# A planner's view of part-tile transfers, the adaptive sums' first term and bias, and the last mixed rows, in a two-layer hybrid DiT kernel on one core

## The chip, the cores and the metric

The kernel runs on one core of a Trainium2 chip. Its time is the device time of one execution in microseconds (us), taken as the median of several runs; a kernel before and a kernel after the change are timed on the same chip. The profile that is read below comes from one further execution with the hardware profiler on.

TensorE is PE in the rows (its weight loads are PEld), VectorE is DVE, ScalarE is ACT, GpSimd is POOL and SyncE is SP. A "q" behind an engine's name (SPq, ACTq) marks the engine's own issuing of DMAs, as against its computing.

## The reference, cut to what matters

Two layers run on 256 latent tokens of width 2048; 256 context tokens join in layer 0. All data are float32.

```python
def reference(x, c, ctx, c_ctx, ada_w, ada_b, norm_g, na_ssd_w_in, ...):
    for i in range(2):
        shift, scale, gate = adaln(c, ada_w[i], ada_b[i])     # silu(c) @ ada_w + ada_b, 3 x 2048
        h = modulate(rms_norm(x, norm_g[i]), shift[:, None], scale[:, None])
        if i == 0:                                            # the context is modulated likewise
            y = na_ssd_mixer(h, hc, ...)                      # one 2048-wide input projection,
                                                              # attention and SSD heads, a group norm,
                                                              # one output projection of [ya, yb]
        else:
            y = short_conv_mixer(h, sc_w_in, sc_conv_w, sc_w_out)
        x = x + gate[:, None] * y
    return x

def short_conv_mixer(h, w_in, conv_w, w_out):
    bg, cg, hv, g = jnp.split(h @ w_in, 4, axis=-1)
    y = bg * dw_conv(cg * hv, conv_w)                         # 3 taps along the tokens
    return (jax.nn.silu(g) * y) @ w_out
```

## The kernel before

**The main stream.** Nearly all of the work is matrix products with weights that are read once. SP brings each weight in pieces of 512 KB into raw buffers (L393). ACT rounds a piece to the short float format of the fast matmul (the CAST to wH, L423), DVE subtracts to get the rest (the TENSOR_TENSOR to wL, L430), and PE multiplies wH by the high and the low part of the activations and wL by the high part (all matmuls are recorded at L198). There are three wH and three wL buffers and five raw ones. A raw buffer is free once its wL is made, and the next load into it is issued then. In layer 1 a piece is worth twelve matmuls of 128x512: eight with wH, four with wL.

**The side work.** Everything else (norms, attention, SSD, convolutions, gates) is written as Python generators that hand out one instruction or a few at a time, in three queues: urgent, side and back. While the kernel is built, a planner (`Plan`, L45 to L135) keeps a clock for each engine and an end time for each written and read piece of a tile, from a table of estimated costs. Before each weight's matmuls, `pump` (L291) asks `may` (L263) for each generator whether the data of its next step would be there in time by these clocks, and if so the step is written into the program at that place. So the planner's clocks set the order in which each engine will execute; on the chip an engine works through its list in that order, and an instruction whose data are late holds up all behind it on its engine. For a DMA, `Plan.add` (L98) takes the start as no earlier than the end of the earlier write to the same piece of the output tile, and sets that piece's end time anew.

**Transfers that fill a tile in parts.** Three places fill one tile by several DMAs: `fetch` (L208 to L213), which reads a 128x2x512 tile by four DMAs of 32 partitions each from the DRAM array trd into Du or Dg, on ACT's queue; the four loads of the attention bias at L1018; and the two loads of exr rows into one tile at L1332. Du and Dg serve layer 1: for each of four column groups `row_gen` (L1755) computes cg * hv, writes it to trd, fetches it back as Du in an order that DVE's 32x32 transposes (`blocks`, L217) turn into channel-major u, and then does the convolution: four multiplications on ACT (L1783) and eight multiply-adds on DVE (L1787, L1789) into v. `gate_gen` (L1793) does the same for the gate with Dg and cg, and multiplies into v and y (L1826 to L1831).

**The adaptive sums.** `gemv_gen` (L805 to L846), in the back queue, computes sixteen blocks of 512 of silu(c) @ ada_w + ada_b on DVE, between the weights. For each block it clears acc (128x512, L810), lets SP put the bias into acc's first row (L811), then adds sixteen products of 512 columns (L820; two per 512 KB piece of ada_w, which uses a raw buffer like a weight). PE sums over the partitions with a matrix of ones, and DVE copies the result to rowb (L829), which ACT's queue writes to the DRAM array mrow.

**The mixed rows.** Layer 0's two head groups make 32 tiles of 128x256. `put_mix` (L936) writes each to the DRAM array mixd on ACT's queue; `mix_gen` (L1528) reads them back two at a time when the room of the old activations is free, and splits them into a high part (ACT) and a low part (DVE) for the output projection. In the group norm, `group_gen` brings the scale r2 (one value per token on the partitions) into a row for all channels: DVE builds two diagonal matrices dg, and PE multiplies ones by them.

## Time and profile before

| | |
|---|---|
| Median of the runs | 1802.93 us (1802.58 to 1804.87, 3 runs) |
| The profiled execution's own time | 1802.22 us |
| Its span, first to last instruction | 1800.3 us |
| Mean granted TensorE clock | 0.998 |
| DMA | 385.23 MB, mean 214 GB/s |
| ACT busy | 785.7 us (44%) |
| POOL busy | 31.1 us (2%) |

The page of the profile gives busy times, the span in 40 slices, and the chain of work that ended last. From the trace behind it come the groups of instructions (count, mean duration, and what ended the idle time before them), the waits by engine, the timeline of a stretch (start, duration, engine, line, operation, the count of instructions drawn together in the row, and in brackets the idle time ahead with what ended it), and the busy times and clock in stretches of one's choice. PE loses 29.3 us in gaps of over 0.3 us between its matmuls; 12.7 us of it is the first load.

### The profile page before, as it was taken

How to read it: one execution, taken by the hardware profiler on the slowest of the kernel's cores; microseconds unless marked ns; L12 is line 12 of the kernel's file. 1: busy time of each engine (PE TensorE's matmuls, PEld its weight loads, DVE VectorE, ACT ScalarE, POOL GpSimd, SP SyncE). 2: the span in 40 equal slices, each digit the busy share in tenths (PEclk: the TensorE clock that was granted, in tenths of full speed). 3: DMA queues.
4: the chain of work that ended last, by engine and by line, in shares of the span. 5: the costliest groups of instructions: out<-in, count | busy, mean ns of one | idle time of the engine just before them, and what ended most of it. 6: DMA issues, size and time to landing. Idle time of an engine off the chain costs nothing.

```text
span 1800.3 us, 25545 instructions
## 1 busy us (share of the span) xinstructions
PE 1760.2 (98%) x9545; PEld 1469.2 (82%) x9545; DVE 1283.5 (71%) x2049; ACT 785.7 (44%) x1354; POOL 31.1 (2%) x28
## 2 busy tenths in 40 slices
PE   6999999999999999999999999999999999999998
PEld 4677888889888879888878898788877888878887
DVE  5566777878686867685875787787657777767555
ACT  5323544436252455242454343554445444434442
POOL 0000100001000000000001000000000000000000
PEclk9999999999999999999999999999999999999999
DMA  9987654576656556655574566768757888878774
GB/s 347 340 291 254 194 168 126 156 206 194 211 161 190 162 174 204 191 158 167 172 219 120 163 188 194 232 209 295 273 184 232 260 278 268 270 237 265 220 220 167
DMA packets 260220, 385.23 MB, mean 214 GB/s; under 512 B 33424, under 2 KB 113008, under 8 KB 260096
## 3 DMA queue, kind: packets, MB, share of 16 engines
q1 hardware_dynamic: 239792, 366.64, 64.8%
q10 hardware_dynamic: 20304, 16.96, 3.1%
q8 instruction: 75, 1.23, 0.3%
q14 instruction: 49, 0.40, 0.1%
HBM read 372.89 MB, written 11.96 MB: 214 GB/s over the span
## 4 chain that ended last, share of the span: by engine, by line
PE 89%; DMA 4%; DVE 4%; issue 1%; ACT 1%; SPq 0%; POOL 0%; ACTq 0%; POOLq 0%; DVEq 0%
PE bank L198 86%; PE bank L202 3%; DMA raw<-in_ada_w 2%; DVE wL L430 2%; DMA tmp<-dram_csr 1%; DVE acc L820 0%; DMA raw<-in_w_in 0%; DMA Dg<-dram_trd 0%; ACT wH L423 0%; DMA tmp<-in_x 0%; DMA xs<-in_x 0%; DVE hL L769 0%; DVE tmp L1398 0%; DVE tmp L1217 0%; DMA Du<-dram_trd 0%
## 5 line engine op out<-in xcount | busy, mean ns | idle before, releaser
L423 ACT CAST wH<-raw 128x1024 fp32r<-128x1024 f32 (+1 forms) x440 | 459.5, 1045 | 707.4 <-PE bank L198 606.5
L430 DVE TENSOR_TENSOR wL<-raw,wH 128x1024 fp32r<-128x1024 f32 (+1 forms) x440 | 530.5, 1212 | 225.9 <-ACT wH L423 224.1
L198 PE MATMUL bank<-hH,wH 128*128 128x256 f32 (+1 forms) x1040 | 342.7, 330 | 0.9 <-ACT wH L423 0.9
L198 PE MATMUL bank<-hL,wH 128*128 128x256 f32 (+1 forms) x1040 | 336.8, 324 | 0.0
L198 PE MATMUL bank<-hH,wL 128*128 128x256 f32 (+1 forms) x1024 | 331.3, 324 | 1.5 <-DVE wL L430 1.5
L198 PE MATMUL bank<-wH,h 128*128 128x512 f32 x1024 | 318.7, 392 | 2.1 <-DVE h L1662 1.7
L198 PE MATMUL bank<-wH,hH 128*128 128x512 f32 x640 | 257.2, 402 | 4.8 <-ACT hH L763 2.6
L820 DVE SCALAR_TENSOR_TENSOR acc<-raw,csil,acc 128x512 f32<-128x512 f32 x256 | 191.7, 749 | 91.0 <-DMA raw<-in_ada_w 74.0
L198 PE MATMUL bank<-wL,hH 128*128 128x512 f32 x640 | 249.8, 391 | 0.3 <-DVE wL L430 0.3
L198 PE MATMUL bank<-wH,hL 128*128 128x512 f32 x640 | 249.5, 390 | 0.1
L198 PEld LDWEIGHTS bank<-wH,h 128*128 128x128 f32 x1024 | 193.0, 189 | 44.3 <-DVE h L1662 3.0
L198 PEld LDWEIGHTS bank<-hH,wH 128*128 128x128 f32 x1040 | 197.6, 190 | 18.7 <-issue 2.0
L198 PEld LDWEIGHTS bank<-hL,wH 128*128 128x128 f32 x1040 | 197.7, 190 | 15.6
L198 PEld LDWEIGHTS bank<-hH,wL 128*128 128x128 f32 x1024 | 194.5, 190 | 17.8 <-DVE wL L430 2.5
L198 PE MATMUL bank<-wL,h 128*128 128x512 f32 x512 | 200.7, 392 | 5.4 <-DVE wL L430 5.4
L198 PE MATMUL bank<-wH,mix 128*128 128x512 f32 x512 | 162.7, 393 | 0.0
L198 PEld LDWEIGHTS bank<-wH,hH 128*128 128x128 f32 x640 | 120.2, 188 | 35.3 <-issue 6.5
L198 PEld LDWEIGHTS bank<-wH,hL 128*128 128x128 f32 x640 | 120.1, 188 | 25.6 <-DVE hL L769 0.6
L198 PEld LDWEIGHTS bank<-wL,hH 128*128 128x128 f32 x640 | 120.2, 188 | 24.8 <-DVE wL L430 1.1
L198 PEld LDWEIGHTS bank<-wL,h 128*128 128x128 f32 x512 | 96.6, 189 | 27.1 <-DVE wL L430 6.9
L198 PEld LDWEIGHTS bank<-wH,mix 128*128 128x128 f32 x512 | 96.1, 188 | 20.8 <-issue 0.9
L198 PE MATMUL bank<-wL,mix 128*128 128x512 f32 x256 | 99.8, 390 | 0.0
(257 smaller groups left out, 1754.4 us busy)
## 6 DMA issues: line engine op xcount, KB each, us to landing
raw<-in_w_in SPq DMA_DIRECT2D x209, 512.0 KB, 3.8
raw<-in_ada_w SPq DMA_DIRECT2D x163, 512.0 KB, 4.7
raw<-in_sc_in SPq DMA_DIRECT2D x128, 512.0 KB, 4.4
raw<-in_w_out SPq DMA_DIRECT2D x64, 512.0 KB, 4.8
raw<-in_sc_out SPq DMA_DIRECT2D x32, 512.0 KB, 4.6
tmp<-dram_csr SPq DMA_DIRECT2D x32, 256.0 KB, 6.2
PT<-in_ada_w SPq DMA_DIRECT2D x14, 512.0 KB, 8.0
yi<-in_ada_w SPq DMA_DIRECT2D x8, 512.0 KB, 7.4
```

The source lines that it names most:

```text
L198: E(T.matmul(o, l, r, start=start, stop=stop, skip_group_check=True))
L202: E(T.transpose(o, i, ident if k == 128 else ident[:k, :k]))
L423: E(S.copy(H, v))
L430: E(V.tensor_tensor(out=Lo, in0=v, in1=H.bitcast(F32), op=ALU.subtract))
L820: E(V.scalar_tensor_tensor(out=acc, in0=v[:, j], scalar=csil[:, 2 * k + j:2 * k + j + 1], in1=acc, op0=ALU.mult, op1=ALU.add))
```

## The change

The diff has five parts.

1. In `Plan.add` a DMA no longer waits in the plan for the earlier write of the same piece, and the piece's end is the later of both. The four DMAs of a fetch or of a bias tile and the two of an exr tile are planned beside each other instead of one after the other.
2. An engine's name may end in "+" (`may`): the data then count as ready 2000 ns later. Used for the products of acc ("DVE+") and for the reading back of mixed rows ("ACT+").
3. `gemv_gen`: no clearing of acc and no bias in acc. The bias goes to a tile adab of its own (128 partitions, four rows used, cleared once), the first product of a block is a TENSOR_SCALAR that writes acc, and the bias is added where the sum leaves its bank for rowb (a TENSOR_TENSOR in place of a COPY).
4. `put_mix` puts a tile straight into its final place (`place`) when the room is free already: eight of the 32 tiles. `mix_gen` reads the others back.
5. `group_gen`: dg and its two matmuls with ones are replaced by two transposes of r2 broadcast to 128x128.

```diff
@@ -105,7 +105,7 @@
         for k in ki:
             s = max(s, self.w[k] + 60)
         for k in ko:
-            s = max(s, 0.0 if e == "PE" else self.w[k] + 60, self.r[k] + 60)
+            s = max(s, 0.0 if e == "PE" or op == "DMACopy" else self.w[k] + 60, self.r[k] + 60)
         if op == "DMACopy":
             n = 4
             for _, c in outs[0].ap:
@@ -128,7 +128,7 @@
             self.r[k] = max(self.r[k], free)
             self.last[k[0]] = max(self.last[k[0]], free)
         for k in ko:
-            self.w[k] = done
+            self.w[k] = max(self.w[k], done) if op == "DMACopy" else done
             self.last[k[0]] = max(self.last[k[0]], done)
         return b
 
@@ -268,8 +268,10 @@
             return grow(task)
         if nb and len(free_b) < nb + (0 if isurg else reserve[0]):
             return False
+        late = eng[-1] == "+"
+        eng = eng.rstrip("+")
         now, t = plan.t["PE"], plan.t["ACT" if eng == "AQ" else eng]
-        rdy = plan.ready(aps)
+        rdy = plan.ready(aps) + (2000 if late else 0)
         if eng == "AQ":
             return t <= now + hor and rdy <= t
         if hor < 2000 and nb and sorted(plan.last[b.tensor.name] for b in free_b)[nb - 1] + 3000 > now:
@@ -329,7 +331,7 @@
                     else:
                         if len(free_b) < nb:
                             continue
-                        when_ = max(plan.t["ACT" if eng == "AQ" else eng], plan.ready(f))
+                        when_ = max(plan.t["ACT" if eng == "AQ" else eng.rstrip("+")], plan.ready(f))
                     if best is None or when_ < best[0]:
                         best = (when_, q, task)
             if best is None:
@@ -806,17 +808,19 @@
         for n in range(16):
             lay = 0 if n < 4 else 1
             c0 = 4096 + n * 512 if n < 4 else (n - 4) * 512
-            yield W_("DVE", nb=0)
-            E(V.memset(acc, 0.0))
-            E(DMA.dma_start(acc[:1, :], ada_b[lay:lay + 1, c0:c0 + 512]))
+            yield W_("SP")
+            E(DMA.dma_start(adab[0:128:32, :], ada_b[lay, c0:c0 + 512].rearrange("(g c) -> g c", g=4)))
             for k in range(8):
                 yield when(lambda: not (("gem", n, k) not in RAW))
-                yield W_("DVE", RAW["gem", n, k][1], acc)
+                yield W_("DVE+", RAW["gem", n, k][1])
                 raw, v = RAW.pop(("gem", n, k))
                 ngem[0] -= 1
                 for j in range(2):
                     if j:
                         yield W_("DVE", acc)
+                    if not k + j:
+                        E(V.tensor_scalar(out=acc, in0=v[:, j], scalar1=csil[:, 0:1], scalar2=None, op0=ALU.mult))
+                        continue
                     E(V.scalar_tensor_tensor(out=acc, in0=v[:, j], scalar=csil[:, 2 * k + j:2 * k + j + 1], in1=acc,
                                              op0=ALU.mult, op1=ALU.add))
                 give_raw(raw)
@@ -826,7 +830,7 @@
             for g in range(4):
                 mm(ps[32 * g:32 * g + 32, :128], ONES[:, :32], acc[:, g * 128:(g + 1) * 128], True, True)
             yield W_("DVE", ps)
-            E(V.tensor_copy(rowb, ps[:, :128]))
+            E(V.tensor_tensor(out=rowb, in0=ps[:, :128], in1=adab, op=ALU.add))
             give(free_b, ps)
             yield W_("AQ", rowb)
             E(DMA2.dma_start(mrow[n // 4, (n % 4) * 512:(n % 4) * 512 + 512].rearrange("(g c) -> g c", g=4), rowb[0:128:32, :]))
@@ -843,6 +847,8 @@
                 n_back[0] = 11.5
 
     rowb = mrb = st([128, 128], "rowb")
+    adab = st([128, 128], "adab")
+    E(G.memset(adab, 0.0))
 
     spawn(back, gemv_gen())
     hold[0] = True
@@ -933,7 +939,20 @@
 
     mixd = drt([32, 128, 256], "mixd")
 
+    mH = [None] * 32
+
+    def place(i, o):
+        hl = st([128, 2, 256], f"hH{i}" if i < 16 else f"hL{i - 16}", F32R, name=f"mix{i}")
+        E(S.copy(hl[:, 0], o))
+        E(V.tensor_tensor(out=hl[:, 1], in0=o, in1=hl[:, 0].bitcast(F32), op=ALU.subtract))
+        mH[i] = hl
+
     def put_mix(i, o):
+        if free_rows[0] > i % 16:
+            yield W_("ACT", o)
+            place(i, o)
+            give(free_h, o)
+            return
         yield W_("AQ", o)
         E(DMA2.dma_start(mixd[i], o))
         give(free_h, o)
@@ -1435,15 +1454,10 @@
         E(V.tensor_scalar(out=r2, in0=pst[:, 0:2], scalar1=1.0 / 256, scalar2=4 * EPS, op0=ALU.mult, op1=ALU.add))
         give(free_b, pst)
         E(G.tensor_tensor(out=r2, in0=r2, in1=mhalf[:, :2], op=ALU.pow))
-        yield W_("DVE", r2)
-        dg = half()
-        for t in range(2):
-            E(V.tensor_scalar(out=dg[:, t * 128:(t + 1) * 128], in0=ident, scalar1=r2[:, t:t + 1], scalar2=None, op0=ALU.mult))
-        yield W_("PE", dg, nb=1)
+        yield W_("PE", r2, nb=1)
         Rb = bank()
         for t in range(2):
-            mm(Rb[:, t * 128:(t + 1) * 128], ONES, dg[:, t * 128:(t + 1) * 128], t == 0, True)
-        give(free_h, dg)
+            turn(Rb[:, t * 128:(t + 1) * 128], r2[:, t:t + 1].to_broadcast([128, 128]))
         yield W_("DVE", Rb)
         for b in range(2):
             i = 2 * g + b
@@ -1523,29 +1537,32 @@
     do_ssd(3, 2)
 
 
-    mH = [None] * 32
-
     def mix_gen(ip):
-        yield when(lambda: 2 * ip in written and 2 * ip + 1 in written and free_rows[0] > (2 * ip + 1) % 16)
-        yield W_("AQ", mixd[2 * ip:2 * ip + 2])
+        two_ = (2 * ip, 2 * ip + 1)
+        yield when(lambda: all(i in written or mH[i] is not None for i in two_) and free_rows[0] > (2 * ip + 1) % 16)
+        mine = [i for i in two_ if mH[i] is None]
+        if not mine:
+            return
+        yield ("grow", 1, 0)
+        yield W_("AQ", *[mixd[i] for i in mine])
         mx = tmp()
         m3 = two(mx)
-        E(DMA2.dma_start(m3, mixd[2 * ip:2 * ip + 2].rearrange("b p c -> p b c")))
-        yield W_("ACT", mx)
-        for j in range(2):
-            i = 2 * ip + j
-            hl = st([128, 2, 256], f"hH{i}" if i < 16 else f"hL{i - 16}", F32R, name=f"mix{i}")
-            E(S.copy(hl[:, 0], m3[:, j]))
-            E(V.tensor_tensor(out=hl[:, 1], in0=m3[:, j], in1=hl[:, 0].bitcast(F32), op=ALU.subtract))
-            mH[i] = hl
+        if len(mine) == 2:
+            E(DMA2.dma_start(m3, mixd[2 * ip:2 * ip + 2].rearrange("b p c -> p b c")))
+        else:
+            E(DMA2.dma_start(m3[:, mine[0] % 2], mixd[mine[0]]))
+        for i in mine:
+            yield W_("ACT+", mx)
+            place(i, m3[:, i % 2])
         give(free_t, mx)
+        yield ("cap", 0, 0)
 
     def mixes(k):
         for ip in order[k::3]:
             yield from mix_gen(ip)
 
     for k in range(3):
-        spawn(urgent, mixes(k), 1)
+        spawn(urgent, mixes(k))
     do_gv(3, 4)
```

The numbers of the lines move by 2 behind `may`, by some 4 behind the adaptive sums, and by 17 in layer 1: the cast of L423 is at L425 after, the transposes stay at L217, the multiplications of L1783 are at L1800.

**Place 1: ACT, layer 1, the first fetch of Du.** Here is ACT's list before, from the writing of trd to the multiplications v that follow the transposes.

```order
L1770 DMA dram_trd<-tmp_108 128x512 [waits DVE_49]
L423 CAST wH_136<-raw_132 128x1024 [waits DMAHW3_49,PE_49,Activation_49]
L423 CAST wH_137<-raw_133 128x1024 [waits DMAHW4_49,PE_49,Activation_49]
L212 DMA Du_11103<-dram_trd 32x8x128 [waits DMAHW6_49,DMAHW0_49]
L212 DMA Du_11103<-dram_trd 32x8x128 x2
L212 DMA Du_11103<-dram_trd 32x8x128 [waits DMAHW1_49]
L423 CAST wH_138<-raw_135 128x1024 [waits DMAHW7_49,DVE_49,PE_49]
L423 CAST wH_136<-raw_131 128x1024 [waits DVE_49,PE_49]
L423 CAST wH_137<-raw_132 128x1024 [waits DMAHW3_49,DVE_49,PE_49]
L423 CAST wH_138<-raw_133 128x1024 [waits DMAHW5_49,DVE_49,PE_49]
L1783 ACTIVATE v<-u,scwh 128x256 [waits DVE_49]
```

And the same stretch of ACT's list after the change.

```order
L1787 DMA dram_trd<-tmp_107 128x512 [waits DMAHW4_49,DVE_49]
L425 CAST wH_138<-raw_131 128x1024 [waits DMAHW7_49,PE_49,Activation_49]
L425 CAST wH_136<-raw_135 128x1024 [waits DMAHW1_49,PE_49,Activation_49]
L212 DMA Du_11052<-dram_trd 32x8x128 [waits DMAHW4_49,DMAHW3_49,DMAHW0_49]
L212 DMA Du_11052<-dram_trd 32x8x128 [waits DMAHW2_49]
L212 DMA Du_11052<-dram_trd 32x8x128 x2
L425 CAST wH_137<-raw_133 128x1024 [waits DVE_49,PE_49]
L425 CAST wH_138<-raw_134 128x1024 [waits DMAHW5_49,DVE_49,PE_49]
L1800 ACTIVATE v<-u,scwh 128x256 [waits DVE_49]
```

Four casts stand between the fetch and the multiplications before, two after. The names in brackets are the semaphores that an instruction waits for.

**Place 2: DVE, layer 1, the third column group.** Here is DVE's list before, ahead of the transposes of Du, where one block of the adaptive sums ends (rowb) and the next begins; raw_134 and raw_133 hold pieces of ada_w in the rows of acc.

```order
L829 COPY rowb<-bank_127 128x128 [waits PE_49]
L810 MEMSET acc 128x512 [waits DVE_49]
L430 TENSOR_TENSOR wL_140<-raw_132,wH_137 128x1024 [waits DMAHW2_49,DVE_49,Activation_49]
L820 SCALAR_TENSOR_TENSOR acc<-raw_134,csil,acc 128x512 [waits DMAHW3_49,DMAHW1_49,DVE_49]
L820 SCALAR_TENSOR_TENSOR acc<-raw_134,csil,acc 128x512 [waits DVE_49]
L430 TENSOR_TENSOR wL_141<-raw_133,wH_138 128x1024 [waits DMAHW4_49,Activation_49]
L820 SCALAR_TENSOR_TENSOR acc<-raw_133,csil,acc 128x512 [waits DMAHW7_49,DVE_49]
L820 SCALAR_TENSOR_TENSOR acc<-raw_133,csil,acc 128x512 [waits DVE_49]
L430 TENSOR_TENSOR wL_139<-raw_135,wH_136 128x1024 [waits DMAHW5_49,Activation_49]
L430 TENSOR_TENSOR wL_140<-raw_131,wH_137 128x1024 [waits DMAHW0_49,Activation_49]
L430 TENSOR_TENSOR wL_141<-raw_132,wH_138 128x1024 [waits DMAHW3_49,Activation_49]
L217 STREAM_TRANSPOSE u<-Du_12257 128x4x4x32 [waits DMAHW4_49,DMAHW6_49,DMAHW1_49,DMAHW0_49]
```

And DVE's list after, from the same group's products hv * cg (L1783) to the transposes.

```order
L1783 TENSOR_TENSOR tmp_107<-bank_123,tmp_113 128x4x4x32 [waits PE_49,Activation_49]
L432 TENSOR_TENSOR wL_141<-raw_134,wH_138 128x1024 [waits DMAHW3_49,Activation_49]
L824 SCALAR_TENSOR_TENSOR acc<-raw_133,csil,acc 128x512 [waits DMAHW5_49,DVE_49]
L824 SCALAR_TENSOR_TENSOR acc<-raw_133,csil,acc 128x512 [waits DVE_49]
L432 TENSOR_TENSOR wL_139<-raw_131,wH_136 128x1024 [waits DMAHW4_49,Activation_49]
L432 TENSOR_TENSOR wL_140<-raw_132,wH_137 128x1024 [waits DMAHW6_49,Activation_49]
L833 TENSOR_TENSOR rowb<-bank_127,adab 128x128 [waits PE_49]
L432 TENSOR_TENSOR wL_141<-raw_135,wH_138 128x1024 [waits DMAHW7_49,Activation_49]
L217 STREAM_TRANSPOSE u<-Du_12193 128x4x4x32 [waits DMAHW5_49,DMAHW7_49,DMAHW1_49,DMAHW0_49]
```

This is what stands behind the transposes after the change (before, the block that follows has begun by then); the eight multiply-adds L1804 and L1806, which read alike, stand between the first of these rows and the second.

```order
L432 TENSOR_TENSOR wL_139<-raw_134,wH_136 128x1024 [waits DMAHW2_49,Activation_49]
L432 TENSOR_TENSOR wL_140<-raw_131,wH_137 128x1024 [waits DMAHW4_49,Activation_49]
L432 TENSOR_TENSOR wL_141<-raw_132,wH_138 128x1024 [waits DMAHW6_49,Activation_49]
L822 TENSOR_SCALAR acc<-raw_133,csil 128x512 [waits DMAHW3_49]
L824 SCALAR_TENSOR_TENSOR acc<-raw_133,csil,acc 128x512 [waits DVE_49]
```

The memset of acc is gone, and the first two products of the new block stand behind the convolution instead of between the weights ahead of the transposes. On ACT's list the fetch of this group stands behind the cast into wH_138 from raw_133 before, and behind the cast into wH_137 from raw_132 after: three wL stand between fetch and transposes before, one after. Counted in the same way over Du and Dg of the four groups, in the order of the program, it is 3, 3, 3, 3, 3, 3, 3, 3 before and 1, 1, 2, 1, 1, 1, 1, 1 after.

## The prediction

> **What bounds the kernel now.** I read the page first, then the waits of PE, then the timeline around each stall.
>
> ```profile
> PE 1760.2 (98%) x9545; PEld 1469.2 (82%) x9545; DVE 1283.5 (71%) x2049; ACT 785.7 (44%) x1354; POOL 31.1 (2%) x28
> PE 89%; DMA 4%; DVE 4%; issue 1%; ACT 1%; SPq 0%; POOL 0%; ACTq 0%; POOLq 0%; DVEq 0%
> PE bank L198 <- DMA raw<-in_ada_w: 12.9, 2, 12.7
> PE bank L198 <- DVE wL L430: 7.2, 7, 4.4
> ```
>
> The busy line and the chain say that PE sets the time: 98% busy, 89% of the chain. So work taken from DVE, ACT or a queue is worth nothing in itself. An edit counts only where PE stands still. The waits of PE (us in total, times, longest) show how little that is: 12.7 us is the first load, which the change doesn't touch, and the largest other item is 7.2 us for wL, of which 4.4 is one stall.
>
> That stall is at 1589 us. Here are DVE's, SP's and PE's rows there (start, duration, engine; in brackets the idle time ahead), and then the stretches with PE's busy time and, as the sixth figure behind the busy times, its clock.
>
> ```profile
> 1582.98 1.54 DVE L820 SCALAR_TENSOR_TENSOR acc<-raw,csil,acc 128x512 f32<-128x512 f32 x2 [2.70 <-DMA acc<-in_ada_b]
> 1585.68 0.37 SPq L393 DMA_DIRECT2D raw<-in_ada_w  x1
> 1590.66 1.54 DVE L820 SCALAR_TENSOR_TENSOR acc<-raw,csil,acc 128x512 f32<-128x512 f32 x2 [5.00 <-DMA raw<-in_ada_w]
> 1592.11 3.49 DVE L430 TENSOR_TENSOR wL<-raw,wH 128x1024 fp32r<-128x1024 f32 x3
> 1593.39 0.80 PE L198 MATMUL bank<-wL,h 128*128 128x512 f32 x1 [4.38 <-DVE wL L430]
> ...
> 1588.60:1591.45 2.85, 0.40 (x2) 0.00 (x0) 0.76 (x2) 1.04 (x1) 0.00 (x0) 1.00 0.19 73
> 1591.45:1593.39 1.94, 0.00 (x1) 0.01 (x1) 1.94 (x3) 0.00 (x0) 0.00 (x0) 0.50 0.08 16
> 1593.39:1598.28 4.89, 4.89 (x12) 3.83 (x13) 3.43 (x4) 0.00 (x0) 0.00 (x0) 0.50 0.98 342
> ```
>
> A new block of the adaptive sums has begun. Its first product waits 2.70 us for the bias in acc, the next piece of ada_w is therefore asked for late (1585.68), and the following product, which the plan has put ahead of three wL, waits 5.00 us for it. PE runs out of wL, idles 4.38 us, and then its granted clock is 0.50 for another 4.89 us of work, half of which is lost: 4.38 + 2.45 = **6.8 us**. A smaller stall of the same kind, and a pair that the adaptive sums help to cause, are these:
>
> ```profile
> 1552.74 1.54 DVE L820 SCALAR_TENSOR_TENSOR acc<-raw,csil,acc 128x512 f32<-128x512 f32 x2 [4.23 <-DMA raw<-in_ada_w]
> 1555.48 0.50 PE L198 MATMUL bank<-wL,h 128*128 128x512 f32 x1 [0.81 <-DVE wL L430]
> 1143.79 0.75 DVE L820 SCALAR_TENSOR_TENSOR acc<-raw,csil,acc 128x512 f32<-128x512 f32 x1 [2.28 <-DMA raw<-in_ada_w]
> 1147.04 0.43 PE L198 MATMUL bank<-tmp,xtm 128*64 128x128 f32 x2 [1.38 <-ACT Vt L989]
> 1148.73 0.65 PE L198 MATMUL bank<-tmp,xtm 128*64 128x128 f32 x6 [1.26 <-DVE tmp L1401]
> ```
>
> **The change part by part.** Its sum is made against the profiled execution's 1802.22 us, of which 1800.3 is the span and 1.92 lies around it; that is 0.7 below the median of the runs, 1802.93.
>
> *The adaptive sums* (parts 2 and 3). Saved on DVE:
>
> ```profile
> L810 DVE MEMSET acc<- 128x512 f32 x16 | 7.8, 485 | 0.9
> L820 DVE SCALAR_TENSOR_TENSOR acc<-raw,csil,acc 128x512 f32<-128x512 f32 x256 | 191.7, 749 | 91.0 <-DMA raw<-in_ada_w 74.0 <-issue 8.2 <-DMA acc<-in_ada_b 5.0
> L1046 DVE TENSOR_SCALAR tmp<-tmp,s 128x512 f32<-128x512 f32 x32 | 15.6, 487 | 1.1
> ```
>
> Sixteen memsets (7.8 us) go, and sixteen products at 749 ns become a TENSOR_SCALAR of the same shape; the nearest row for that has 487 ns, so 16 x 0.26 = 4.2 us. That is 12 of DVE's 1283.5 us, and DVE has 500 us of idle time: nothing by itself. The worth lies in the waits. The 5.0 us for the bias and the 74.0 us for ada_w are idle times that stand ahead of wL on DVE. With the 2000 ns that "+" adds, the plan puts a product later behind the load of its piece. In the third group (place 2) the block's first products now stand behind the convolution and wait for no bias. So I take the stalls at 1589 and 1555 as gone: -6.8 - 0.8 = **-7.6**; of the pair at 1147 (2.6 us) most, with a little elsewhere: **-2**. Bounds: 0, if the products find a new place just as bad, and -12.2, if also the rest of the 7.2 us goes (2.0) and all of the pair (0.6).
>
> *Side-by-side transfers, Du and Dg* (part 1). This is where I see a loss. The plan used to add the four DMAs of a fetch, and now takes the latest of four; so it believes that the tile is there earlier, and puts the transposes after one weight instead of three (place 1 and 2). What the transfer really takes is in the trace. The rows of one undisturbed fetch, the last Du, with the casts and wL of the three weights, and then of the second Du, where DVE came early enough to see the landing:
>
> ```profile
> 1672.67 1.83 ACTq L212 DMA_DIRECT2D Du<-dram_trd  x4
> 1675.27 1.05 ACT L423 CAST wH<-raw 128x1024 fp32r<-128x1024 f32 x1 [1.62 <-PE bank L198]
> 1676.36 1.23 DVE L430 TENSOR_TENSOR wL<-raw,wH 128x1024 fp32r<-128x1024 f32 x1 [1.45 <-ACT wH L423]
> 1677.99 1.05 ACT L423 CAST wH<-raw 128x1024 fp32r<-128x1024 f32 x1 [1.67 <-PE bank L198]
> 1682.94 1.30 DVE L217 STREAM_TRANSPOSE u<-Du 128x512 f32<-128x512 f32 x2
> 1683.43 1.06 ACT L423 CAST wH<-raw 128x1024 fp32r<-128x1024 f32 x1 [1.67 <-PE bank L198]
> 1684.13 0.39 PE L198 MATMUL bank<-wL,h 128*128 128x512 f32 x1
> 1685.66 0.48 DVE L1787 SCALAR_TENSOR_TENSOR v<-u,scwh,v 128x255 f32<-128x255 f32 x1
> 1689.31 2.35 DVE L430 TENSOR_TENSOR wL<-raw,wH 128x1024 fp32r<-128x1024 f32 x2
> ...
> 1493.37 2.11 ACTq L212 DMA_DIRECT2D Du<-dram_trd  x4
> 1502.85 1.30 DVE L217 STREAM_TRANSPOSE u<-Du 128x512 f32<-128x512 f32 x2 [0.58 <-DMA Du<-dram_trd]
> ```
>
> The landing comes 1502.85 - 1493.37 = 9.5 us after the first issue: at 1682.2 in the first stretch. A weight lasts 2.72 us (casts at 1675.27 and 1677.99). After the change DVE has made one wL by 1676.36 + 1.23 = 1677.6, and then stands before the transposes until 1682.2, **4.6 us**, with the next wL queued behind them, and behind that the convolution, the next wL, and on ACT the casts behind v. Follow it on: transposes to 1683.5, next wL (1.22) to 1684.7. The cast of that weight is the one at 1677.99; three buffers mean that PE begins it two weights later, at 1683.43, and reads its wL first at 1684.13. PE waits 0.6. Then the eight multiply-adds, 1689.31 - 1685.66 = 3.65, to 1688.4, and the wL after that to 1689.6, due at 1684.13 + 0.6 + 2.72 = 1687.45: PE waits 2.15 more. **2.8 us for each Du** with one weight between (three of four); the one with two weights has 2.72 more time, and I take 0.3. 3 x 2.8 + 0.3 = **+8.7**.
>
> The Trainium skill ("DMA: Bandwidth & Descriptors", Anatomy of one DMA) gives the fixed part of one DMA, on GpSimd's path, as about 2.0 us, most of it the confirmation that the last byte is written. An estimate by that page: the last issue 1.4 us after the first, 2.0 us and some bytes, so about 4 us; DVE, there after 4.9, would not wait and this term would be nothing. The row with 0.58 in brackets says 9.5 on this queue, and the measurement decides.
>
> For Dg the steps are shorter: behind the transposes only one product of 0.43 stands ahead of the next wL.
>
> ```profile
> 1724.29 1.83 ACTq L212 DMA_DIRECT2D Dg<-dram_trd  x4
> 1729.67 1.05 ACT L423 CAST wH<-raw 128x1024 fp32r<-128x1024 f32 x1 [1.67 <-PE bank L198]
> 1735.95 0.43 DVE L1826 TENSOR_TENSOR v<-cg,v 128x256 f32<-128x256 f32 x1
> ...
> 1458.88 2.41 ACTq L212 DMA_DIRECT2D Dg<-dram_trd  x4
> 1470.49 1.30 DVE L217 STREAM_TRANSPOSE cg<-Dg 128x512 f32<-128x512 f32 x2 [1.49 <-DMA Dg<-dram_trd]
> ...
> Dg<-dram_trd ACTq DMA_DIRECT2D x16, 128.0 KB, 7.5
> ```
>
> At the median of 7.5 us behind an issue, the last issue (1.83 less one of four, 1.4 after the first) lands at 1733.2; transposes 1.30, product 0.43, wL 1.22 end at 1736.15. It is due two weights and 0.7 after the cast at 1729.67: 1729.67 + 5.44 + 0.7 = 1735.8. So 0.35 to 0.4 each, 4 x 0.4 = **+1.6**. But a fetch waits for its two halves in trd, and the first Dg landed 11.6 us after its first issue, 2.7 later than this; with DVE already waiting such a lateness goes straight to PE. I take it once: **+2.5**. Together +12.8. Bounds: +4, if PE's queue of weights is deeper than I count at the Du (each 1.5 less) and no fetch is late; +20, if three of eight are late by 2.5.
>
> *Bias and exr tiles* (part 1). They too are used sooner after their issues.
>
> ```profile
> bias<-dram_rpbs SPq DMA_DIRECT2D x64, 64.0 KB, 3.7
> L1018 SPq DMA_DIRECT2D bias<-dram_rpbs x64: 579/614/1811, 229.3 to 1166.4; - x64
> L1023 DVE TENSOR_TENSOR bias<-bias,const 128x512 f32<-128x512 f32 x16 | 11.0, 686 | 1.2 <-DMA bias<-dram_rpbs 1.2
> ```
>
> Three issues of 0.6 us (614 ns) ahead of the last and 3.7 to land make 5.5 us; DVE waits 1.2 us for it in 16 tiles now, and stands up to 2 us longer when one to two weights fewer lie between. In layer 0 a wait of DVE under 2 us mostly dies in the three wL buffers, as these 1.2 us do: no wait of PE leads back to a bias tile. **+1**, bounds 0 and 4.
>
> *Mixed rows, r2* (parts 4 and 5). Eight writes to mixd and four reads back go, two dg products and two matmuls become two transposes per group; all of it beside PE's stream, whose matmul count stays. That is nothing, with the weights' casts and the 500 idle us of DVE as cover. That the whole order of layer 0 shifts by some instructions is worth nothing I can sign: bounds -3 and +3.
>
> Sum: -7.6 - 2 + 12.8 + 1 = **+4.2** on 1802.2, or about **1807** on the runs' median.
>
> **The rivals.**
>
> *Faster: the new waits are hidden.* If DVE's 4.6 us in front of Du cost PE nothing (or the transfers land sooner, being asked for amid lighter traffic), the gains stand alone: 1802.9 - 7.6 - 2 + 1, and 1 for what is left of the waits, is 1795. For it: three pieces of wL are the buffer, and no idle time of PE now is put down to Du or Dg. Against it: 1493.37 and 1458.88 measure the landing, and eight multiply-adds stand directly behind.
>
> *No change: the two cancel.* At the low bound of the Du waits (+4 to +8): 1798 to 1803. Nothing in the rows speaks for exact cancelling, but the terms are of like size.
>
> *Clearly slower: the new stalls take the clock with them.* The place is behind the convolution of Du, where PE idles 0.6 and then 2.15 us; the point is the share of idle time at which the clock falls. Above, the clock fell at 1591.45, in a stretch of 2.85 us in which PE worked 0.40, and PE then worked at half speed for 4.89 us; the idle times of 1.38 and 1.26 at 1147 left it at full. 2.15 lies between. If it falls at three Du, each costs about 2.4 to 3.4 us more: 1807 + 3 x 3 = 1816. The Trainium skill ("TensorE: Matmul & The Clock Gate", What's actually happening) says that the clock halves after an idle window of about 3.4 us, whose phase doesn't depend on the kernel. By that rule 2.15 us would not do it, and this rival would be worth nothing; but the trace shows a fall after less than a whole idle window (0.40 us busy in it), so I keep it.
>
> *The change doesn't do what it says:* a product of acc on a raw buffer given back one or two weights earlier still waits for the landing, and a stall like that at 1589 comes back elsewhere: 1807 + 4 to 7 = 1811 to 1814.
>
> **How the numbers follow.** The forecast, gains of some 10 against waits of some 13 to 15: 0.42, about 1803 to 1811. Waits hidden: 0.18, 1793 to 1799. Cancelling: 0.18, 1799 to 1803. Clock falls: 0.12, 1811 to 1818. Stalls of acc come back: 0.10, 1809 to 1816. The range 1796 to 1817 leaves out the far ends of the first and the third case. A measurement of this kernel can tell about 0.2%, 3.6 us: faster (under 1799.3) 0.19; same (to 1806.5) is the cancelling and a good third of the forecast, 0.32; slower 0.49.
>
> **What would show it.** Right: no L820 row with 5.00 in brackets, PE's wait for wL made of pieces of 2 to 3 us behind the transposes of Du, and a wait of 4 to 5 us for Du in front of three of four. Wrong: transposes that wait under 2 us, which would mean that the fetch is issued earlier than the lists suggest or lands faster; or clocks of 0.5 behind Du. A stall in layer 0 of over 3 us, or a product of acc that waits over 4 us ahead of wL, would mean that the order moved in a way that I did not follow.

## The result, and the profile after

| | before | after |
|---|---|---|
| Median of the runs | 1802.93 us (1802.03 to 1804.87, 5 runs) | 1812.26 us (1808.81 to 1814.56, 5 runs) |
| The profiled execution's own time | 1802.22 us | 1808.81 us |
| Its span | 1800.3 us | 1807.0 us |

The ratio after to before is 1.005, with a 95% interval of 1.0035 to 1.0065: the change makes the kernel slower by 9 us. The forecast was 1807, slower by 4, with a range that reaches to 1817.

The page of the profile after, its line of busy times and its chain by engine, then from the trace the waits of PE (us in total, times, longest), and DVE's for the fetched tiles, the products and the bias:

```profile
PE 1759.6 (97%) x9529; PEld 1466.1 (81%) x9529; DVE 1269.9 (70%) x2017; ACT 786.7 (44%) x1354; POOL 31.3 (2%) x29
PE 79%; DMA 9%; DVE 7%; ACT 2%; issue 2%; SPq 1%; ACTq 0%; POOL 0%; DVEq 0%; POOLq 0%
PE bank L198 <- DVE wL L432: 14.9, 14, 2.0
PE bank L198 <- DMA raw<-in_ada_w: 13.8, 2, 13.6
PE bank L198 <- DVE tmp L1420: 1.4, 1, 1.4
DVE acc L824 <- DMA raw<-in_ada_w: 15.2, 16, 2.9
DVE u L217 <- DMA Du<-dram_trd: 14.6, 4, 4.7
DVE cg L217 <- DMA Dg<-dram_trd: 13.3, 4, 3.9
DVE bias L1042 <- DMA bias<-dram_rpbs: 11.8, 8, 3.0
```

DVE has 14 us less to do, and PE's work is the same but for 16 small matmuls; yet the span is 6.7 us longer. By the rows of the two traces PE's gaps of over 0.3 us sum to 39.9 us, against 33.1 before (the 29.3 given further up is too low); 0.9 of the difference is the first load. The chain shows the same: PE's share fell from 89% to 79%, and DMA (4% to 9%) and DVE (4% to 7%) took most of the ten. The one stall of 4.4 us for wL is gone; where there were seven stalls for wL, 7.2 us in all, there are now fourteen of at most 2.0, 14.9 us in all. The products' waits for ada_w fell from 74.0 to 15.2 us. In their place DVE waits 14.6 us for Du and 13.3 us for Dg, at every one of the eight fetches; before, these waits were 0.6 and 1.5 us.

One of the places, the first Du: DVE's and ACT's rows, PE's two rows with idle time ahead of them, and then two stretches (length, the busy times of PE, PEld, DVE, ACT and POOL, the granted clock, the share of DMA and its GB/s).

```profile
1399.75 1.86 ACTq L212 DMA_DIRECT2D Du<-dram_trd  x4
1403.00 1.22 DVE L432 TENSOR_TENSOR wL<-raw,wH 128x1024 fp32r<-128x1024 f32 x1 [1.45 <-ACT wH L425]
1404.14 0.74 DVE L824 SCALAR_TENSOR_TENSOR acc<-raw,csil,acc 128x512 f32<-128x512 f32 x1
1408.08 1.31 DVE L217 STREAM_TRANSPOSE u<-Du 128x512 f32<-128x512 f32 x2 [3.20 <-DMA Du<-dram_trd]
1409.31 1.18 DVE L432 TENSOR_TENSOR wL<-raw,wH 128x1024 fp32r<-128x1024 f32 x1
1410.55 0.50 PE L198 MATMUL bank<-wL,h 128*128 128x512 f32 x1 [0.29 <-DVE wL L432]
1414.08 2.35 DVE L432 TENSOR_TENSOR wL<-raw,wH 128x1024 fp32r<-128x1024 f32 x2
1415.35 0.50 PE L198 MATMUL bank<-wL,h 128*128 128x512 f32 x1 [1.79 <-DVE wL L432]
...
1412.70:1416.77 4.07, 2.28 (x10) 1.58 (x9) 4.00 (x7) 1.37 (x2) 0.00 (x0) 1.00 0.29 90
1416.77:1420.19 3.42, 3.42 (x10) 2.69 (x9) 1.46 (x2) 0.93 (x1) 0.00 (x0) 0.50 0.97 326
```

One wL behind the fetch, then the wait for the landing, then the two stalls of PE, the small one ahead of the convolution and the large one behind it. The clock of 0.50 for 3.42 us after it, all of them work, costs another 1.7.

### The profile page after: what moved, and what is told of

Same layout as the page of the kernel before. It is cut to its first block, busy times and chain, and to the rows that moved or that the text cites. A ratio compares the mean times of both kernels' runs of the same rounds, so it can differ in the third digit from the quotient of the medians.

```text
span 1807.0 us, 25441 instructions
## 1 busy us (share of the span) xinstructions
PE 1759.6 (97%) x9529; PEld 1466.1 (81%) x9529; DVE 1269.9 (70%) x2017; ACT 786.7 (44%) x1354; POOL 31.3 (2%) x29
## 4 chain that ended last, share of the span: by engine, by line
PE 79%; DMA 9%; DVE 7%; ACT 2%; issue 2%; SPq 1%; ACTq 0%; POOL 0%; DVEq 0%; POOLq 0%
PE bank L198 76%; DMA tmp<-dram_csr 3%; DVE wL L432 3%; PE bank L202 2%; DMA raw<-in_sc_in 1%; ACT wH L425 1%; DMA dram_trd<-tmp 1%; DMA Dg<-dram_trd 1%; DMA Du<-dram_trd 1%; DMA raw<-in_ada_w 1%; DMA bias<-dram_rpbs 1%; SPq L1037 0%; DVE acc L824 0%; ACTq L212 0%; DVE tmp L1406 0%
## 5 line engine op out<-in xcount | busy, mean ns | idle before, releaser
L425 ACT CAST wH<-raw 128x1024 fp32r<-128x1024 f32 (+1 forms) x440 | 459.0, 1045 | 652.1 <-PE bank L198 593.7
L824 DVE SCALAR_TENSOR_TENSOR acc<-raw,csil,acc 128x512 f32<-128x512 f32 x240 | 179.8, 749 | 19.2 <-DMA raw<-in_ada_w 15.2
```

Source lines behind the costliest of these rows:

```text
L425: E(S.copy(H, v))
L824: E(V.scalar_tensor_tensor(out=acc, in0=v[:, j], scalar=csil[:, 2 * k + j:2 * k + j + 1], in1=acc, op0=ALU.mult, op1=ALU.add))
```

## The experiments

The theory (A) is the prediction's: by the side-by-side rule the plan believes in a landing that comes too early, and DVE waits. The rivals are named in the expectations, which were written before each run. Times of one group were taken on one chip beside the kernel before; the ratio is against that.

| kernel | parts of the change in it | median, us | range | ratio to before, 95% interval |
|---|---|---|---|---|
| after | 1 to 5 | 1812.26 | 1808.81 to 1814.56 | 1.005 (1.0035 to 1.0065) |
| e1_plan_undone | 2 to 5 | 1793.21 | 1790.47 to 1797.89 | 0.9943 (0.9925 to 0.9962) |
| e2_plan_alone | 1 | 1832.48 | 1825.84 to 1836.41 | 1.0154 (1.0123 to 1.0185) |
| e3_landing | 1 to 5, landing of fetch +5000 ns | 1792.05 | 1790.90 to 1793.43 | 0.9934 (0.9916 to 0.9952) |
| e4_fetch_serial | 2 to 5, 1 for SP only | 1794.39 | 1793.17 to 1796.09 | 0.9947 (0.9929 to 0.9966) |
| b1_plus_alone | 2 (acc) | 1817.33 | 1816.13 to 1818.78 | 1.0076 (1.0061 to 1.0091) |
| b2_bias_alone | 3 | 1801.02 | 1797.81 to 1805.36 | 0.9982 (0.9970 to 0.9994) |
| b3_sums | 2 (acc), 3 | 1804.49 | 1800.55 to 1808.02 | 1.0007 (0.9997 to 1.0017) |
| b4_no_mixed | 2 (acc), 3, 5 | 1806.15 | 1800.99 to 1810.49 | 1.0006 (0.9990 to 1.0022) |
| b5_mixed_alone | 4 (with its 2000 ns) | 1821.79 | 1819.77 to 1825.09 | 1.0098 (1.0076 to 1.0120) |
| e7_landing_less | 1 to 5, landing of fetch +2000 ns | 1797.36 | 1790.97 to 1798.51 | 0.9949 (0.9929 to 0.9969) |
| e6_sp_serial | 2 to 5, 1 for ACT's queue only, landing +5000 ns | 1788.82 | 1787.74 to 1790.63 | 0.9913 (0.9898 to 0.9929) |

### The plan's rule undone, alone, and with a true landing

```diff
 e1: (on the changed kernel)
-            s = max(s, 0.0 if e == "PE" or op == "DMACopy" else self.w[k] + 60, self.r[k] + 60)
+            s = max(s, 0.0 if e == "PE" else self.w[k] + 60, self.r[k] + 60)
-            self.w[k] = max(self.w[k], done) if op == "DMACopy" else done
+            self.w[k] = done
 e2: the same lines the other way round, on the kernel before
 e3: (on the changed kernel, with the rule)
-                done = free = max(self.dma, s + 1000) + n / self.RATE + 1500
+                done = free = max(self.dma, s + 1000) + n / self.RATE + 1500 + (5000 if ins[0].tensor.name.startswith("dram_trd") else 0)
 e4: as e1, but both lines keep the rule where e == "SP"
```

> The changed kernel with its first part alone undone: the plan again lets a DMA wait for the earlier write of the same piece. By the order of the program three weights stand between fetch and transposes again in all eight fetches. Theory A (the side-by-side rule makes DVE wait for Du and Dg, and this is the whole loss): DVE's waits before the transposes fall under 1.5 us, the stalls of PE behind them (13.9 us in the profile after) go, and the time is 1793 to 1798 us, faster than the kernel before by 5 to 10. Rival B (the shifted order of the other four parts costs the time): 1807 to 1813, as the changed kernel. Rival C (the gains at 1589 and elsewhere came from the side-by-side rule too): about 1803, as before.

1793.21 us: as A has it, and clear of B and C. What the other four parts bring without the rule is ten us, as in the forecast's faster rival (1795). DVE's one wait for Du that is left, PE's waits for wL, and one row of DVE:

```profile
DVE u L217 <- DMA Du<-dram_trd: 0.9, 1, 0.9
PE bank L198 <- DVE wL L432: 2.9, 4, 2.1
...
1491.28 1.54 DVE L824 SCALAR_TENSOR_TENSOR acc<-raw,csil,acc 128x512 f32<-128x512 f32 x2 [5.36 <-DMA raw<-in_ada_w]
```

DVE doesn't wait for Dg at all, and no stall of PE is left behind a fetch that comes from such a wait. The one stall of 2.1 us comes from a product of acc that stands ahead of the landing of ada_w, as at 1589 before: that kind is not gone.

> The kernel before with the first part of the change alone. One weight stands between fetch and transposes in all eight. Theory A: 2.8 us for each of four Du and 0.4 to 2 for each Dg more, 13 to 17 us, and the adaptive sums keep their stalls, perhaps at other places: 1812 to 1822 us. Rival B: 1801 to 1805. Theory A also says that the stall of 4.4 us at 1589 may move, since the order of the first products against the transposes moves, so a time of 1808 to 1812 would show the 6.8 us gone by the move alone.

1832.48 us: the direction is A's, but 10 us past its upper end. Two rows of DVE from the trace of e2, two of PE's waits, and the sum over the four stretches in which the clock was 0.50 (from 697.17, 1164.80, 1243.31 and 1618.77) show what I had not counted:

```profile
1426.91 1.30 DVE L217 STREAM_TRANSPOSE u<-Du 128x512 f32<-128x512 f32 x2 [4.57 <-DMA Du<-dram_trd]
1246.06 0.76 DVE L1539 TENSOR_TENSOR mix<-tmp,mix 128x256 fp32r<-128x256 f32 x2 [6.00 <-ACT mix L1538]
...
PE bank L198 <- DVE wL L430: 19.5, 14, 4.1
PE bank L198 <- ACT mix L1538: 5.7, 1, 5.7
...
sum 20.48, PE 16.05 PEld 13.67 DVE 12.78 ACT 3.83 POOL 3.90; mean PE 4.01 PEld 3.42 DVE 3.19 ACT 0.96 POOL 0.97
```

Du waits as A says, and PE's gaps behind the eight fetches sum to 13.5 us. But a pair of mixed rows read back at the end of layer 0 also comes late now, and PE stands 5.7 us for it; at 695 it stands 4.1 us for wL behind two bias tiles. And behind these stalls PE worked 16.05 us at a clock of 0.50, where it was 4.89 before: 8.0 us lost instead of 2.4.

> The changed kernel, with all of its parts, but the plan counts 5000 ns more until a DMA that reads trd has landed (about what the trace shows). Theory A (not the rule, but the landing that the plan believes in is wrong): three weights stand between fetch and transposes, and the time is within 3 us of the kernel with the plan undone, 1793 to 1799 us. Rival B: 1807 to 1813. If the side-by-side planning of the bias and exr tiles costs time too, it stays here: up to 4 us above the kernel with the plan undone.

1792.05 us. With the rule in, and only the landing set to about what the trace shows, the loss is gone. So it isn't the rule as such but the landing that it implies.

> The changed kernel with the side-by-side rule kept for SP's DMAs (bias and exr tiles) and undone for ACT's queue (Du, Dg). Theory A: 1793 to 1799 us; its difference from the kernel with the whole rule undone is the price of the bias and exr tiles, which I put at 1 us with bounds 0 and 4. A time near 1808 would mean that these tiles, not Du and Dg, make the loss.

1794.39 us: Du and Dg make the loss, not the tiles of bias and exr. The price of those, the difference to e1, is 1.2 us, within what two medians can differ by here; e6 below asks again.

### How many weights between

e7 has e3's line with 2000 in the place of 5000.

> The changed kernel, with 2000 ns more (instead of 5000) until a DMA that reads trd has landed. Two weights stand between fetch and transposes in all eight, against one (1812 us) and three (1792 us). I took 0.3 us for a Du with two weights, since 2.72 us of the wait of 4.6 fall away: by that the eight fetches cost 1 to 4 us, 1792 to 1797 us, with waits of 1 to 3 us in front of the transposes of Du. If the loss goes by the share of weights, it is 1799 to 1804.

1797.36 us (ratio 0.9949): 0.4 above the upper end of the one and under the other. One, two and three weights give 1812, 1797 and 1792 us; by the ratios, as the three were timed beside different runs of the kernel before, two weights lie 3 us above three, and their intervals overlap. In the profile of e7 DVE's waits are 6.1 us for the four Du (at most 2.2) and 5.1 for the four Dg, and PE's gaps behind them sum to 1.1 us, less than I had sized. But the profiled execution, 1790.97, was the lowest of the six; one of the others, 1798.28, had the same granted clock (0.999), so most of that loss is not the clock. What it is, is not shown.

### The changed kernel once more

> The changed kernel once more, for its profile. Its runs lie between 1808.81 and 1814.56 and the profiled one was the lowest. Theory H (the stalls of about 2 us behind Du and Dg drop the granted clock in some executions and places and not in others): this execution shows the same gaps of PE within 1 us, and its time differs from 1808.81 by about half of the difference in time at clock 0.50 (one stretch of 3.4 us, at 1416.8, in the first profile). Rival J (the landings vary): the clock shows the same, and the waits in front of Du and Dg carry the difference.

1808.47 us, within 0.4 us of the first profile, but made up otherwise. DVE's waits for the fetches in this trace, PE's rows at the same first Du, and the stretch there:

```profile
DVE u L217 <- DMA Du<-dram_trd: 15.9, 4, 4.4
DVE cg L217 <- DMA Dg<-dram_trd: 14.4, 4, 4.3
1410.24 0.50 PE L198 MATMUL bank<-wL,h 128*128 128x512 f32 x1 [0.88 <-DVE wL L432]
1415.04 0.50 PE L198 MATMUL bank<-wL,h 128*128 128x512 f32 x1 [1.77 <-DVE wL L432]
1405.00:1425.00 20.00, 17.35 (x81) 13.33 (x80) 13.83 (x21) 7.81 (x10) 0.00 (x0) 1.00 0.63 205
```

PE idles as long there (1.77 us) and the clock stays at 1.00. DVE's waits for the fetches are longer by 2.4 us in sum, and PE's gaps behind them sum to 13.8 us, against 12.2 in the first profile. The first profile has a second stretch at half speed that the expectation had not seen, at 27.55 us, 3.41 long and all work; this one has neither. So both H and J move the time: PE's busy time is 1.3 us shorter here (1758.3 against 1759.6) and its gaps in the whole kernel are 1.0 longer. Two executions say no more than that.

### The adaptive sums alone

b1 is the kernel before with `"DVE+"` for the products and the two lines of `may` and `force` that read it; b2 has the whole of part 3 and `"DVE"`; b3 has both.

> The kernel before with the 2000 ns for the products of acc alone (memset and bias in acc stay, no side-by-side rule). Theory P (the stalls at 1555 and 1589 come from products that are put ahead of the landing of ada_w): no product of acc waits over 3 us ahead of a wL, and the time is 1793 to 1797 us. Theory Q (they come from the bias that is loaded into acc): the first product of a block still waits about 2.7 us and the stall stays, 1799 to 1803.

> The kernel before with the third part alone: no memset, the bias added at the eviction, the first product a TENSOR_SCALAR, without the 2000 ns. Theory Q: the 6.8 us at 1589 go, 1794 to 1798 us. Theory P: a product still waits 4 to 5 us for ada_w somewhere in layer 1 and PE with it, 1799 to 1804.

> The kernel before with both edits of the adaptive sums, without the side-by-side rule and without the edits of the mixed rows and of r2. If the latter two are worth nothing, as I put them, the time is that of the changed kernel with the plan undone (1793.2 us), within 2 us: 1791 to 1796. If they are worth something, it lies at 1797 to 1802.

The times are 1817.33, 1801.02 and 1804.49. The first and the last lie outside every theory; the second is in P's range, but without the wait of PE that P asked for. In all three the stall of 4.4 us at 1589 is gone. Its kind is not: in b1 a product still waits 5.67 us for ada_w and PE 2.4 us for wL behind it (at 1691), in b3 5.48 and 4.63 us with 2.2 and 1.4 of PE (at 1501 and 1593); b2 has none over 0.8. So P's clause for b1, that no product waits over 3 us, fails, and so does Q's, that the stall stays where the bias stays. Which edit took the stall at 1589 away, or whether the shifted order did, is not shown. For the order of all else moved too, and at the end of layer 0 a new stall stands. Here it is in b1, ACT's and DVE's rows and PE's wait:

```profile
1238.39 1.12 ACTq L940 DMA_DIRECT2D dram_mixd<-half  x2
1246.48 0.38 ACTq L1535 DMA_DIRECT2D tmp<-dram_mixd  x1
1249.04 0.71 ACT L1540 CAST mix<-tmp 128x256 fp32r<-128x256 f32 x2 [14.21 <-DMA tmp<-dram_mixd]
1249.48 0.76 DVE L1541 TENSOR_TENSOR mix<-tmp,mix 128x256 fp32r<-128x256 f32 x2 [10.06 <-ACT mix L1540]
...
PE bank L198 <- ACT mix L1540: 11.7, 1, 11.7
```

The last two rows are written to DRAM at 1238, read back at 1246 and cast at 1249, with ACT and DVE standing before them. PE idles 11.7 us, and the clock of 0.50 behind it, over 5.58 us of work, costs another 2.8. In b3 the same place has a gap of 4.0 us, in b2 two of 1.4 and 1.5.

### The mixed rows

b4 is e1 with part 4 undone as well, and with it the 2000 ns for the rows that are read back and the changed calls around `mix_gen`; b5 is the kernel before with the same edits alone. What each of these three is worth was not run.

> The changed kernel with its first part (the plan) and its fourth part (the mixed rows) undone: the adaptive sums and r2 stay. With both sums' edits alone the time was 1804.5 us, with all but the plan 1793.2; parts 4 and 5 must hold the 11 us. Theory M (a late read of mixed rows from DRAM holds ACT ahead of a cast at the end of layer 0, 4.1 us of idle PE and 6.8 us at half clock in the profile of the sums alone, and part 4 takes it away): 1801 to 1807 us, with such a wait of ACT. Theory N (r2 by transposes gives it): 1791 to 1796.

1806.15 us, with 6.0 us of PE idle for mixed rows at 1233: Theory M. Against e1, of another group, part 4 is worth 11 (by the ratios) to 13 us here; against b3, part 5 (r2 by transposes) is worth nothing that two ranges of 7 to 10 us can show.

```profile
1230.63 0.42 ACTq L1534 DMA_DIRECT2D tmp<-dram_mixd  x1
1238.69 0.71 ACT L1539 CAST mix<-tmp 128x256 fp32r<-128x256 f32 x2 [4.42 <-DMA tmp<-dram_mixd]
1239.15 0.80 PE L198 MATMUL bank<-wH,mix 128*128 128x512 f32 x1 [5.96 <-ACT mix L1539]
```

This stall and 5.0 us of work at half speed behind it cost 8.5 us. They are not all of the difference: in b4's profile PE also stands 2.7, 2.2 and 2.5 us for wL (at 1147, 1505 and 1597), and the clock falls behind all three; e1 has one such stall, of 2.1 us, and no fall. The two at 1505 and 1597 come behind products that wait 5.41 and 5.79 us for ada_w.

> The kernel before with the fourth part alone (mixed rows placed without DRAM where there is room, and the 2000 ns for those read back). The trace before shows no wait of PE for mixed rows, so Theory M, which calls the part a guard against a stall that the order before happens not to have, gives 1800 to 1805. If the part is worth something by itself (fewer transfers, fewer instructions on ACT's queue), 1793 to 1798.

1821.79 us, which no theory had. There is no late mixed row from DRAM at the end of layer 0, but the products of acc now stand ahead of the landing of ada_w in new places, worse than before. DVE's rows in layer 1, and PE's waits for wL:

```profile
1429.67 1.54 DVE L822 SCALAR_TENSOR_TENSOR acc<-raw,csil,acc 128x512 f32<-128x512 f32 x2 [5.27 <-DMA raw<-in_ada_w]
1610.17 1.54 DVE L822 SCALAR_TENSOR_TENSOR acc<-raw,csil,acc 128x512 f32<-128x512 f32 x2 [8.11 <-DMA raw<-in_ada_w]
PE bank L198 <- DVE wL L432: 18.9, 9, 6.5
```

So each edit alone leaves the other weakness open, and a new order finds it. Parts 2 to 5 together (e1) close the one at the end of layer 0; of the products they leave one wait of 5.36 us, with a stall of 2.1.

### A version that beats both

e6 keeps the rule for ACT's queue with e3's landing, and plans SP's part-tile DMAs one after the other.

> The changed kernel with the side-by-side rule for ACT's queue alone, with 5000 ns more to the landing of a DMA that reads trd; SP's part-tile DMAs (bias, exr) planned one after the other as before. The stall of 2 us at 695 behind two bias tiles, which the runs with the rule for SP have and the run without it has not, should go: 1788 to 1792 us. If it makes no difference, 1791 to 1794.

1788.82 us, 0.9913 of before: the lowest median of all. The stall at 695 is gone, and PE waits for wL 0.9 us in the whole kernel. It lies 3 us under e3; but the two were timed on different chips, and the intervals of their ratios overlap, so that it is faster than e3 is likely and not shown. PE's and DVE's waits:

```profile
PE bank L198 <- DVE wL L432: 0.9, 4, 0.3
DVE u L217 <- DMA Du<-dram_trd: 0.8, 2, 0.6
```

## Why the prediction was right, and where not

*The sum, +4.2.* The side is right and the size is half: 9 us slower where 4 was said. 1812 lies inside the range, but just above the 1803 to 1811 of the forecast's own case and in the ranges of two rivals, and neither of these came about as told: the clock fell behind one Du, not three, and no product of acc waited over 2.9 us.

*What bounds the kernel.* Right: PE with few gaps, and DVE's 14 us less were worth nothing in themselves.

*The adaptive sums, -7.6 and -2.* Right as a sum: e1 shows -9.8 against the kernel before of its group (1793.21 to 1803.05). The places are right too: in e1 the stalls at 1589 and 1555 are gone, and of the pair at 1147 0.9 us is left. That it held is luck in part. I gave the gain to parts 2 and 3; together and without the rest (b3) they are worth nothing (1804.49 against 1803.99), part 3 alone brings 3 us (b2) and part 2 alone loses 13 (b1), since the order that they make lets the last mixed rows come late. And the reason, that a product behind the landing of its piece no longer holds up wL, holds only where the order happens to allow it: the longest wait of a product is 2.9 us in the changed kernel, but 5.36 in e1 and 5.79 in b4, which have the same two parts.

*The mixed rows, "nothing that I can sign".* This is the step that failed. I looked for the wait in the trace of before, found none, and priced the part at nothing. It is a guard: b4 and e1 differ by this part and its 2000 ns alone, and by 13 us in their medians (11 by their ratios to before), of which the stall that it guards against is 8.5 in b4's profile; alone (b5) it loses 17. The trace of one order says nothing about the stalls that another order has.

*Du and Dg, +12.8.* The mechanism is right: one wL behind the fetch, a wait of DVE for the landing, then a small stall of PE and a larger one behind the convolution. The sum is right as well for the profiled execution: PE's gaps behind the eight fetches are 12.2 us, 8.1 for Du against the 8.7 of the text and 4.1 for Dg against 4.1. But it came out by luck, since the single fetches differ. These are the second Du, the one with two weights, and the last, with one:

```profile
1505.42 1.30 DVE L217 STREAM_TRANSPOSE u<-Du 128x512 f32<-128x512 f32 x2 [4.66 <-DMA Du<-dram_trd]
1507.88 0.50 PE L198 MATMUL bank<-wL,h 128*128 128x512 f32 x1 [0.67 <-DVE wL L432]
1512.68 0.50 PE L198 MATMUL bank<-wL,h 128*128 128x512 f32 x1 [1.79 <-DVE wL L432]
...
1684.68 1.31 DVE L217 STREAM_TRANSPOSE u<-Du 128x512 f32<-128x512 f32 x2 [2.05 <-DMA Du<-dram_trd]
1691.94 0.50 PE L198 MATMUL bank<-wL,h 128*128 128x512 f32 x1 [0.60 <-DVE wL L432]
```

The text gave 0.3 us to the first of them and 2.8 to the other; they cost 2.5 and 0.6, as the one landed 10.8 us after its issue and the other 7.0. Waits of 4 to 5 us stood in front of two of the four Du, not three.

As a price of the rule the term is too small: the changed kernel lies 19 us above e1 and 20 above e3. Between the profiled executions of the changed kernel and of e1 it is 18.3 us. Of these, 13.1 are gaps of PE: 12.2 behind the fetches and 2.0 at 695 behind two bias tiles, less 1.1 net at other places. The other 5.3 are PE's busy time for the same 9529 matmuls, of which 3.4 are the two stretches at half speed; the cause of the rest is not shown. The median lies another 3.5 us above the profiled execution, the lowest of its five. It can hardly be the clock: the run at the median, and one at 1813.91, have the same mean granted clock, 0.998, as the one at 1808.81, and 0.001 of it is 1.8 us. Later landings, as in the second profile, may be it; that stays open.

*Bias and exr, +1.* Probably too small: DVE waits 11.8 us for bias where it waited 1.2, and PE loses 2.0 us at 695, which the text had as nothing. e4 against e1 puts it at 1, e6 against e3 at 3 to 4, both within the bounds of 0 and 4 and neither clear of the noise.

*The clock rival.* Given 0.12, as an all or nothing at three Du. It came at one of the four Du in one execution and at none in another.

## What to carry to other kernels

Where a plan made before the run sets the order, a term that it has too large may be holding up another that it has too small: four DMAs one after the other, at the 3.0 us that `Plan.add` gives to one of 128 KB, made 12 us for a tile that lands after 7 to 11; side by side they made 4 to 5. Before making such an estimate truer in one term, compare its sum with the landings in the trace. And test the parts of such a change together and each left out, not each alone: alone, an edit mostly shows which order it happens to fall into (parts 1, 2, 3 and 4 by themselves gave +29, +13, -3 and +17 us; 2 to 5 together -10).

## What the runs showed of the hardware

The clock fell to 0.50 after PE had idled 1.79 us, in a stretch of 4.07 us in which it worked 2.28, and stayed there for 3.42 us; at an idle time of 1.77 us in the same place of another execution it stayed at 1.00. In the fourteen traces, from 100 us on, six of 23 idle times of PE of 1.48 to 2.10 us were followed by a stretch at half speed, and all but one (2.97 us, in e2) of the 19 from 2.15 to 11.66 us; the stretches last 3.41 us, 6.83 or, once, 17.07. The first profile of the changed kernel also has one at 27.55 us, behind idle times that all the others have at that place without it. So idle times of about 2 us may or may not cost a stretch at half speed. Long stalls are paid for a second time in this way: PE worked 12 to 18 us at half speed in e2, b1, b4 and b5, and not at all in e1, e6 and e7. The Trainium skill ("TensorE: Matmul & The Clock Gate", What's actually happening) has the clock halve after an idle window of about 3.4 us with a phase of its own; the length of the half-speed stretch agrees with its window, the idle time doesn't, and the measurement decides. The fetch of Du, four DMAs of 128 KB each, landed 8.3, 10.8, 9.0 and 7.0 us after its first issue in the four groups of one execution: one number for a landing, even a measured one, leaves some of them late.
